# A hybrid encoder block on one Trainium2 core: 128-row attention scores, layer norm statistics ahead of attention, a reordered first norm, and one-hot operations that read their rows from PSUM

## The chip, the cores and the metric

One core of one Trainium2 chip runs the whole kernel as one program. The metric is the device time of one execution in microseconds (us). The engines are TensorE (PE in the profile; PEld is its weight load), VectorE (DVE), ScalarE (ACT), GpSimd (POOL) and SyncE (SP), each with its own instruction queue, worked off in order.

## The reference

For 512 tokens of width 1024, in float32:

```
h = RMSNorm(x);  z = h @ w_in        # columns: GLU 2x1024 | q 16x64 | k 4x64 | v 4x64 | gates 2x1024
A = swish(LayerNorm(conv31(glu)) ) @ w_pw
B = windowed GQA(q, k, v; |t-s| <= 128, ALiBi bias, per-head sink) @ w_o
x = x + (sigmoid(gA) * A + sigmoid(gB) * B) @ w_out
x = x + PEER(RMSNorm(x))             # 8 heads, top 16 of 128 x 128 experts, gelu(u.h) * gate, weighted sum of v rows
out = RMSNorm(x)
```

PEER takes, per token and head, the top 16 of 128 first keys and of 128 second keys, then the top 16 of their sums; each winner is one of 16384 experts.

## The kernel before

**Number format.** Each float32 operand of a projection is split into a high part (ScalarE copy, `split`, L57) and a remainder (L58, on DVE or POOL), and each product is three matmuls (`mm3`, L63 to L65).

**First norm (L140 to L154).** A hand-ordered section: ScalarE, VectorE and SyncE keep program order. Four 128-token tiles of x are loaded; ScalarE takes each sum of squares, VectorE the reciprocal and the scaling; the first weight block is loaded and split; ScalarE loads the sigmoid table; then `spread` transposes on TensorE into `psn` and writes hT as high (ACT L102) and low part (DVE L103).

**Branches (L189 to L331).** `glu(i)` makes two projections into the two PSUM buffers `s` of pool `psa`, which lies where `psn` lay. `conv` is 31 multiply-adds per pair of channel blocks on VectorE. The key tiles `kh`, `kl` hold two key groups each, one in rows 0 to 63 and one in rows 64 to 127. `attend(g, b)` is called 16 times (4 groups, 4 query blocks): per head a score product of 64 contraction rows (L264), maximum and bias (L267), exponentials (ACT L275), division by the denominator (DVE L285 for two heads, ACT L283 for two), transposes (L290), and the product with v (`o`). `fill` puts gate projections between them.

**Layer norm of the convolution (L333 to L355)** follows attention: means by matmul with `ones` (L337), centring (L342), squares (ACT L344), variance by matmul (L345), Sqrt, reciprocal over 512 columns (L348), scaling (DVE L350), Silu (ACT L352), split. Then the projections with w_o, w_pw and w_out (`oraw`).

**PEER.** `u_block(i)` loads 128 experts' u rows, splits them (ACT, POOL `ulo`) and makes 24 matmuls of 384 columns into `hps`; 30 of them (`LEAD`) run ahead of the second half. Meanwhile VectorE does the top-k. `build(t)`, for three of the four token tiles, turns the chosen pairs into a dense gate matrix: indices and gates are transposed into `tp`, written as 2-byte pairs into `tt`, and for each 8 tokens VectorE makes `oij` (2048 columns, compare with an iota, L607) and `ohl` (two multiplies of 1024 columns, L609), from which 16 matmuls make two `gp` tiles (L615, L616), evicted by ScalarE (L618) and written to DRAM. There are 3 x 16 such steps. Afterwards `v_block(i)` combines hidden values and v rows for all 128 expert blocks, with the remaining u blocks and, for token tile 0, 256 row gathers beside it.

**Order.** Outside the hand-ordered sections a planner orders each engine's instructions by dependencies, program order and its own cost estimates; `tc.high_priority()` moves an instruction forward. [...]

Of the kernel before, what the change touches and what calls it, by code (L numbers as in the profile page):

```python
# [44 lines left out]
def encoder_block(ctx, tc, x, g1, w_in, taps, dwb, lng, lnb, w_pw, sink, w_o, w_out, g2, g2row,  # L45
# [71 lines left out]
    with ExitStack() as fc:  # L117
# [15 lines left out]
        with ExitStack() as x0c:  # L133
            x0 = x0c.enter_context(tc.tile_pool(name="x0", bufs=1))
            hT_hi, hT_lo = bigtile(), bigtile()
            psn = x0c.enter_context(tc.tile_pool(name="psn", bufs=6, space=PSUM))
            xt, xs = [], []
            vec = {"g1": const.tile([P, KD], F32, name="g1")}
            ordered = {mybir.EngineType.Activation, mybir.EngineType.DVE, mybir.EngineType.SP}
            with tc.manual_schedule(engines=ordered):  # L140
                ACT.activation(warm, epst, AF.Sqrt)
                for t in range(NT):
                    a = x0.tile([P, D], F32, name="xt", bufs=NT)
                    (SP if t % 2 else ACT).dma_start(a, x[t * P:(t + 1) * P, :])
                    xt.append(a)
                SP.dma_start(vec["g1"], g1)
                for t in range(NT):
                    xn = x0.tile([P, D], F32, name="xn", bufs=NT)
                    rs = rstd_of(xt[t], sm, xn)
                    scale_row(xn, xt[t], rs)  # L150
                    xs.append(xn)
                first = weights(w_in[0])
                ACT.activation(warm, rs, AF.Sigmoid)
                spread(xs, vec["g1"], psn, hT_hi, hT_lo, 0)  # L154
            for name, src in (("dwb", dwb), ("lng", lng), ("lnb", lnb), ("g2", g2)):
                vec[name] = const.tile([P, KD], F32, name=name)
                POOL.dma_start(vec[name], src)
            tapt = const.tile([P, KD, TAPS], F32, name="tapt")
            POOL.dma_start(tapt, taps)
            sinkt = const.tile([P, NH], F32, name="sinkt")  # L160
            POOL.dma_start(sinkt, bcast(sink, NH))
            keyt = const.tile([P, 2, NKEY], F32, name="keyt")
            POOL.dma_start(keyt, keys)
# [12 lines left out]
        with ExitStack() as ac:  # L176
            kvp = ac.enter_context(tc.tile_pool(name="kvp", bufs=1))
            kh = kvp.tile([P, 2, S], F32R, name="kh")
            kl = kvp.tile([P, 2, S], F32R, name="kl")
            vh = kvp.tile([P, NT, 2 * P], F32R, name="vh")  # L180
            vl = kvp.tile([P, NT, 2 * P], F32R, name="vl")
            dist = kvp.tile([P, 3 * P], F32, name="dist")
            aw = ac.enter_context(tc.tile_pool(name="aw", bufs=2))
            psa = ac.enter_context(tc.tile_pool(name="psa", bufs=2, space=PSUM))
# [4 lines left out]
            def glu(i):  # L189
                pa = proj(w_in[i], hT, first if i == 0 else None, ps=psa.tile([P, S], F32, name="s"))  # L190
                pg = proj(w_in[8 + i], hT, ps=psa.tile([P, S], F32, name="s"))
# [23 lines left out]
            for i in range(2):  # L215
                ps = proj(w_in[24 + i], hT)
                with tc.high_priority():
                    split(kh[:, i, :], kl[:, i, :], ps, DVE)
            vps = psa.tile([P, 2, 2, P], F32, name="pt", bufs=2)
            vps2 = psa.tile([P, 2, 2, P], F32, name="pt", bufs=2)  # L220
            vt = []
            for i in range(2):
                ps = proj(w_in[26 + i], hT)
                a = aw.tile([P, 4, 3 * P], F32, name="L", bufs=3).rearrange("p a b -> p (a b)")[:, :S]
                ACT.activation(a, ps, AF.Copy)
# [27 lines left out]
            def attend(g, b):  # L253
# [8 lines left out]
                for i in range(4):  # L262
                    s_ps = psa.tile([P, S], F32, name="s")
                    mm3(s_ps[:, :n], [(qh[rows, gp * 4 + i, cols], ql[rows, gp * 4 + i, cols])],  # L264
                        [(kh[rows, gp, k0 * P:k1 * P], kl[rows, gp, k0 * P:k1 * P])])
                    h = 4 * g + i
# [14 lines left out]
                for i in range(4):  # L281
                    if i % 2:
                        ACT.activation(L[:, i, :n], L[:, i, :n], AF.Copy, scale=rd[:, i:i + 1])  # L283
                    else:
                        DVE.tensor_scalar(L[:, i, :n], L[:, i, :n], rd[:, i:i + 1], None, op0=OP.mult)  # L285
                o_ps = pso.tile([P, 4, P], F32, name="o")
# [12 lines left out]

            dtmp = aw.tile([P, 4, 3 * P], F32, name="L", bufs=3)[:, 0, :]  # L300
            POOL.iota(dist, pattern=[[-1, 3 * P]], base=P, channel_multiplier=1,
# [22 lines left out]
            fill(2)  # L324
            glup.close()
            pso = ac.enter_context(tc.tile_pool(name="pso", bufs=1, space=PSUM))
            for g in range(4):
                make_bias(g)
                for b in range(NT):
                    attend(g, b)  # L330
                    if b == 1 or (g, b) == (0, 3):  # L331
                        fill(1)
            lnp = ac.enter_context(tc.tile_pool(name="lnp", bufs=2))  # L333
            ac_hi, ac_lo = bigtile(), bigtile()
            mu_ps = pso.tile([P, S], F32, name="ln")
# [11 lines left out]
            ACT.activation(rs, var, AF.Sqrt, bias=epst)  # L347
            DVE.reciprocal(rs, rs)  # L348
            for k in range(KD):
                DVE.tensor_tensor(cv[:, k, :], cv[:, k, :], rs, op=OP.mult)  # L350
                act = lnp.tile([P, S], F32, name="act", bufs=2)
                ACT.activation(act, cv[:, k, :], AF.Silu, scale=vec["lng"][:, k:k + 1],  # L352
# [93 lines left out]
    with ExitStack() as rc:  # L446
# [374 lines left out]
```

## Time and profile before

| | us |
|---|---|
| median of 3 runs | 1814.74 (1811.3 to 1815.37) |
| the profiled execution | 1812.98 |
| its span in the trace | 1811.2 |

Busy shares of the span: PE 96%, PEld 82%, DVE 79%, POOL 53%, ACT 43%. A matmul's record is longer than the distance to the next one, since matmuls overlap; a full PE share therefore does not say that PE runs at its peak, and the distance from start to start is what a matmul costs in a dense row. "Idle before" names what ended an engine's wait. PEclk (and the column of that name in the table by stretches) is the granted TensorE clock as a share of full speed.

### The profile page before, as it was taken

What the parts mean: (1) busy time and instruction counts of PE and PEld (TensorE: products, weight loads), DVE (VectorE), ACT (ScalarE), POOL (GpSimd) and SP (SyncE); (2) the same over time, 40 slices, a digit from 0 to 9 for tenths busy, and PEclk for the clock granted to TensorE, in tenths of its full rate; (3) what the DMA queues carried; (4) which work ended last, traced back from release to release, by engine and by line L of the source; (5) the groups of instructions that cost most, each with busy time, mean ns of one, the idle gap of its engine ahead of it and who ended that gap; (6) DMA issues with size and microseconds to landing.
All of it is one profiled execution on the core that took longest, in us unless ns stands there. A gap on an engine that the chain in (4) does not pass through costs nothing.

```text
span 1811.2 us, 25192 instructions
## 1 busy us (share of the span) xinstructions
PE 1734.4 (96%) x8873; PEld 1484.2 (82%) x8873; DVE 1432.8 (79%) x2545; ACT 770.8 (43%) x1374; POOL 961.4 (53%) x741
## 2 busy tenths in 40 slices
PE   6999999989999978888999999999999999999998
PEld 5778877658888877767899999999999999999876
DVE  4999856674536999999989987887787777878874
ACT  4233257883343335555443433333333333333243
POOL 4444421020134445445448888778777778778511
PEclk8999999999999989999999999999999999999999
DMA  4223210024243113777878988888888888898972
GB/s 142 87 92 100 98 59 24 24 82 152 81 148 100 56 59 124 233 214 227 290 257 321 333 309 328 311 318 312 313 317 304 323 317 315 295 332 287 343 259 93
DMA packets 148942, 379.42 MB, mean 209 GB/s; under 512 B 11520, under 2 KB 63760, under 8 KB 148816
## 3 DMA queue, kind: packets, MB, share of 16 engines
q1 hardware_dynamic: 110832, 241.20, 38.1%
q0 software_dynamic: 37120, 134.52, 20.8%
q10 hardware_dynamic: 864, 2.10, 0.3%
q8 instruction: 69, 1.13, 0.2%
q14 instruction: 57, 0.47, 0.1%
HBM read 346.84 MB, written 30.93 MB: 209 GB/s over the span
## 4 chain that ended last, share of the span: by engine, by line
PE 68%; DVE 15%; issue 2%; DMA 2%; ACT 1%; POOL 1%; SPq 0%; POOLq 0%; DVEq 0%; ACTq 0%
PE acc L64 8%; PE acc L63 8%; PE acc L65 8%; PE hps L65 7%; PE hps L64 7%; PE hps L63 7%; PE mm L63 5%; PE mm L65 5%; PE mm L64 4%; DVE ohl L609 4%; DVE oij L607 3%; DMA row<-in_v_dram,eidx 1%; PE s L63 1%; PE pt L290 1%; PE s L64 1%
## 5 line engine op out<-in xcount | busy, mean ns | idle before, releaser
L58 POOL TENSOR_TENSOR ulo<-uraw,uhi 128x512 fp32r<-128x512 f32 x256 | 406.1, 1595 | 290.6 <-ACT uhi L57 271.0
L63 PE MATMUL hps<-big,uhi 128*128 128x384 f32 x1024 | 349.3, 341 | 2.2 <-ACT hb L442 2.1
L65 PE MATMUL hps<-big,ulo 128*128 128x384 f32 x1024 | 349.4, 341 | 0.9 <-POOL ulo L58 0.9
L64 PE MATMUL hps<-big,uhi 128*128 128x384 f32 x1024 | 349.0, 341 | 0.0
L64 PE MATMUL acc<-vlo,ph 128*128 128x512 f32 x768 | 300.7, 392 | 1.6 <-DVE vlo L58 1.6
L65 PE MATMUL acc<-vhi,pl 128*128 128x512 f32 x768 | 299.6, 390 | 0.0
L63 PE MATMUL acc<-vhi,ph 128*128 128x512 f32 x768 | 299.1, 391 | 0.4 <-ACT vhi L57 0.4
L58 POOL TENSOR_TENSOR wlo<-wraw,whi 128x512 fp32r<-128x512 f32 x120 | 157.8, 1318 | 203.5 <-ACT whi L57 202.0
L57 ACT ACTIVATE uhi<-uraw 128x512 fp32r<-128x512 f32 x256 | 160.1, 631 | 233.6 <-PE hps L64 140.9
L643 DVE SCALAR_TENSOR_TENSOR row<-row,h2tok 128x1024 f32<-128x1024 f32 x128 | 189.5, 1487 | 66.4 <-DMA row<-in_u_dram,eidx 66.3
L654 DVE SCALAR_TENSOR_TENSOR yacc<-row,dots,yacc 128x1024 f32<-128x1024 f32 x127 | 177.2, 1396 | 69.7 <-DMA row<-in_v_dram,eidx 69.4
L58 DVE TENSOR_TENSOR vlo<-vraw,vhi 128x1024 fp32r<-128x1024 f32 x128 | 188.6, 1474 | 18.9 <-ACT vhi L57 18.9
L636 POOL DMA_INDIRECT row<-in_u_dram,eidx x128 | 183.8, 1436 | 33.2 <-issue 21.1
L63 PEld LDWEIGHTS hps<-big,uhi 128*128 128x128 f32 x1024 | 194.3, 190 | 6.6 <-ACT hb L442 2.5
L64 PEld LDWEIGHTS hps<-big,uhi 128*128 128x128 f32 x1024 | 194.6, 190 | 4.2
L57 ACT ACTIVATE whi<-wraw 128x512 fp32r<-128x512 f32 x152 | 95.3, 631 | 239.2 <-PE mm L64 125.5
L65 PEld LDWEIGHTS hps<-big,ulo 128*128 128x128 f32 x1024 | 194.2, 190 | 2.0 <-POOL ulo L58 1.9
L636 POOL DMA_INDIRECT row<-in_v_dram,eidx x128 | 165.1, 1290 | 48.7 <-DVE yacc L654 21.5
L57 ACT ACTIVATE ph<-hb 128x384 fp32r<-128x384 f32 x128 | 66.8, 523 | 287.4 <-PE acc L64 274.6
L65 PEld LDWEIGHTS acc<-vhi,pl 128*128 128x128 f32 x768 | 144.2, 188 | 30.9 <-DVE pl L58 0.3
L64 PEld LDWEIGHTS acc<-vlo,ph 128*128 128x128 f32 x768 | 144.2, 188 | 30.0 <-DVE vlo L58 3.7
L63 PEld LDWEIGHTS acc<-vhi,ph 128*128 128x128 f32 x768 | 144.1, 188 | 28.4 <-ACT vhi L57 1.0
(221 smaller groups left out, 3211.7 us busy)
## 6 DMA issues: line engine op xcount, KB each, us to landing
uraw<-in_ut_dram SPq DMA_DIRECT2D x128, 512.0 KB
vraw<-in_v_dram SPq DMA_DIRECT2D x128, 512.0 KB
gates_dram<-st SPq DMA_DIRECT2D x12, 2048.0 KB
gt<-gates_dram SPq DMA_DIRECT2D x32, 768.0 KB
wraw<-in_w_in_dram SPq DMA_DIRECT2D x44, 512.0 KB
wraw<-in_w_query_dram SPq DMA_DIRECT2D x16, 512.0 KB
wraw<-in_w_o_dram SPq DMA_DIRECT2D x8, 512.0 KB
oraw<-in_w_out_dram SPq DMA_DIRECT2D x16, 256.0 KB
```

The lines of the kernel that those rows point to most:

```text
L57: ACT.activation(hi, src, AF.Copy)
L58: lo_engine.tensor_tensor(lo, src, f(hi), op=OP.subtract)
L63: PE.matmul(ps, wh, mh, start=first and i == 0, stop=False)
L64: PE.matmul(ps, wh, ml, start=False, stop=False)
L65: PE.matmul(ps, wl, mh, start=False, stop=last and i == n - 1)
L290: PE.transpose(pt[:, i, :], L[:, i, j * P:(j + 1) * P], ident)
L607: DVE.tensor_tensor(prs(oij), iota8, rows(0), op=OP.is_equal)
L609: DVE.tensor_tensor(prs(ohl)[:, s * TB8:(s + 1) * TB8], prs(oij)[:, TB8:], rows(2)[:, s * TB8:(s + 1) * TB8], op=OP.mult)
L636: POOL.indirect_dma_start(out=row, out_offset=None, in_=table, in_offset=bass.IndirectOffsetOnAxis(ap=eidx[:, c:c + 1], axis=0))
L643: DVE.scalar_tensor_tensor(row, row, 1.0, h2tok, op0=OP.mult, op1=OP.mult, accum_out=dots[:, c:c + 1])
L654: DVE.scalar_tensor_tensor(yacc, row, dots[:, c:c + 1], yacc, op0=OP.mult, op1=OP.add)
```

## The change

- First norm: the fourth tile's sum of squares goes to VectorE; the three others, all roots, the reciprocals and the scalings are written in another order; the split of the first weight block is put into the transpose loop after steps 1 and 4 and the sigmoid table load after it; the first projection goes to the pool `psm`.
- Keys: `kh`, `kl` get one slot of 128 rows for each of the four groups, the other group's 64 rows are zeroed by POOL, and the score products contract over 128 rows. The key split becomes two of 64 rows each.
- Two of four divisions per `attend` go from ACT to POOL. The pool `aw` (score and bias tiles) is opened after the convolution.
- The layer norm's statistics go ahead of attention; its scaling (8 tiles) goes to POOL, between the calls of `attend` for g = 1 and 2. Silu writes in place.
- `build`: ScalarE copies `tt` bit by bit into a PSUM tile `tq`; `oij` and `ohl` read their rows there; `ohl` is one operation of 2048 columns. [...]

```diff
@@ first norm
-                for t in range(NT):
-                    xn = x0.tile([P, D], F32, name="xn", bufs=NT)
-                    rs = rstd_of(xt[t], sm, xn)
-                    scale_row(xn, xt[t], rs)
-                    xs.append(xn)
-                first = weights(w_in[0])
-                ACT.activation(warm, rs, AF.Sigmoid)
-                spread(xs, vec["g1"], psn, hT_hi, hT_lo, 0)
...
+                DVE.scalar_tensor_tensor(xs[3], xt[3], 1.0, xt[3], op0=OP.mult, op1=OP.mult, accum_out=sss[3])
+                raw0 = wst.tile([P, KD, P], F32, name="wraw", bufs=3)
+                SP.dma_start(raw0.rearrange("p k c -> p (k c)"), w_in[0])
+                for t in (0, 1, 2, 3):
+                    if t < 3:
+                        ACT.activation(xs[t], xt[t], AF.Square, accum_out=sss[t])
+                    ACT.activation(sss[t], sss[t], AF.Sqrt, scale=1.0 / D, bias=epst)
...
+                for k in range(KD):
+                    tp = psn.tile([P, S], F32, name="mm")
...
+                    if k in (1, 4):
...
+                        split(hi, lo, raw0[:, q * n:(q + 1) * n, :], POOL)
...
+                ACT.activation(warm, epst, AF.Sigmoid)
@@ keys and scores
-            kh = kvp.tile([P, 2, S], F32R, name="kh")
-            kl = kvp.tile([P, 2, S], F32R, name="kl")
+            kh = kvp.tile([P, 4, S], F32R, name="kh")
+            kl = kvp.tile([P, 4, S], F32R, name="kl")
+            for a in (kh, kl):
+                POOL.memset(f(a[64:, 0::2, :]), 0.0)
+                POOL.memset(f(a[:64, 1::2, :]), 0.0)
...
-                pa = proj(w_in[i], hT, first if i == 0 else None, ps=psa.tile([P, S], F32, name="s"))
+                pa = (proj(w_in[0], hT, first) if i == 0 else
+                      proj(w_in[i], hT, ps=psa.tile([P, S], F32, name="s")))
...
-                    split(kh[:, i, :], kl[:, i, :], ps, DVE)
+                    for r in range(2):
+                        rr = slice(64 * r, 64 * r + 64)
+                        split(kh[rr, 2 * i + r, :], kl[rr, 2 * i + r, :], ps[rr], DVE)
...
-                    mm3(s_ps[:, :n], [(qh[rows, gp * 4 + i, cols], ql[rows, gp * 4 + i, cols])],
-                        [(kh[rows, gp, k0 * P:k1 * P], kl[rows, gp, k0 * P:k1 * P])])
+                    mm3(s_ps[:, :n], [(qh[:, gp * 4 + i, cols], ql[:, gp * 4 + i, cols])],
+                        [(kh[:, g, k0 * P:k1 * P], kl[:, g, k0 * P:k1 * P])])
...
-                    if i % 2:
-                        ACT.activation(L[:, i, :n], L[:, i, :n], AF.Copy, scale=rd[:, i:i + 1])
-                    else:
-                        DVE.tensor_scalar(L[:, i, :n], L[:, i, :n], rd[:, i:i + 1], None, op0=OP.mult)
+                    (POOL if i % 2 else DVE).tensor_scalar(L[:, i, :n], L[:, i, :n], rd[:, i:i + 1], None,
+                                                           op0=OP.mult)
@@ layer norm: L335 to L348 now stand ahead of this loop
+            def ln_scale(k):
+                POOL.tensor_tensor(cv[:, k, :], cv[:, k, :], rs, op=OP.mult)
...
+                    attend(g, b)
+                    if g in (1, 2):
+                        ln_scale(4 * (g - 1) + b)
...
-                DVE.tensor_tensor(cv[:, k, :], cv[:, k, :], rs, op=OP.mult)
@@ build
-            tp = psg.tile([P, 3, P], F32, name="tp", bufs=1)
+            tp = psg.tile([P, 4, P], F32, name="gp", bufs=4)
...
+            tq = psg.tile([P, 512], F32, name="tq", bufs=2)
+            ACT.activation(tq, tt.rearrange("p g s t b -> p (g s t b)").bitcast(F32), AF.Copy)
+            tqv = tq.bitcast(F16).rearrange("p (g s t b) -> p g s t b", s=4, t=TB8, b=2)
...
-                        a = tt[:, n // TB8, s:s + 2].rearrange("p s t b -> p (s t) b")
+                        a = tqv[:, n // TB8, s:s + 2].rearrange("p s t b -> p (s t) b")
...
-                    for s in range(2):
-                        DVE.tensor_tensor(prs(ohl)[:, s * TB8:(s + 1) * TB8], prs(oij)[:, TB8:],
-                                          rows(2)[:, s * TB8:(s + 1) * TB8], op=OP.mult)
+                    jj = oij[:, 1].rearrange("p t (a b) -> p t a b", b=2)
+                    DVE.tensor_tensor(ohl.rearrange("p s t (a b) -> p s t a b", b=2),
+                                      jj[:, None].to_broadcast([P, 2, TB8, NKEY // 2, 2]),
+                                      rows(2).rearrange("p (s t) a b -> p s t a b", s=2), op=OP.mult)
...
-                        gp = psg.tile([P, 4, NKEY], F32, name="gp", bufs=5)
+                        gp = psg.tile([P, 4, NKEY], F32, name="gp", bufs=4)
```

## Rows read from the trace of the kernel before

**Rows 1.** The page, busy time by engine, and its costliest POOL group of the weight splits.

```profile
PE 1734.4 (96%) x8873; PEld 1484.2 (82%) x8873; DVE 1432.8 (79%) x2545; ACT 770.8 (43%) x1374; POOL 961.4 (53%) x741
...
L58 POOL TENSOR_TENSOR wlo<-wraw,whi 128x512 fp32r<-128x512 f32 x120 | 157.8, 1318 | 203.5 <-ACT whi L57 202.0
```

**Rows 2.** Busy time by stretch: start:end, length, each engine's busy time (count), clock, DMA.

```profile
243.00:367.40 124.40, 124.36 (x579) 87.18 (x578) 80.99 (x265) 98.43 (x238) 9.05 (x7) 1.00 0.08 26
367.40:406.80 39.40, 33.35 (x126) 21.32 (x124) 29.92 (x48) 34.19 (x67) 10.51 (x8) 0.96 0.31 94
...
685.00:855.00 170.00, 140.30 (x1233) 118.18 (x1232) 169.88 (x261) 86.97 (x166) 79.25 (x47) 0.98 0.65 199
855.00:875.00 20.00, 19.59 (x112) 18.95 (x110) 19.30 (x76) 11.13 (x19) 10.92 (x11) 1.00 1.04 348
1000.00:1200.00 200.00, 200.00 (x1014) 182.33 (x1013) 172.61 (x201) 75.57 (x120) 165.91 (x113) 1.00 0.87 320
```

**Rows 3.** Timeline of the start, ScalarE: start, length, line, operation, count.

```profile
14.79 4.71 ACT L102 ACTIVATE big<-mm,g 128x512 fp32r<-128x512 f32 x8
```

**Rows 4.** Timeline of the start, TensorE: the first projection's first matmul.

```profile
20.91 0.79 PE L63 MATMUL s<-big,whi 128*128 128x512 f32 x1 [2.64 <-DVE big L103]
```

**Rows 5.** Timeline of TensorE in attention: the first and the last run of 64-row scores.

```profile
243.46 0.38 PE L63 MATMUL s<-kh,qh 64*128 64x256 f32 x1
...
363.20 0.40 PE L64 MATMUL mm<-ql,whi 128*128 128x512 f32 x1
363.44 0.43 PE L63 MATMUL o<-ph,vh 128*128 128x512 f32 x1
363.80 0.38 PE L63 MATMUL s<-kh,qh 64*128 64x256 f32 x1
364.02 0.28 PE L64 MATMUL s<-kl,qh 64*128 64x256 f32 x1
...
364.49 0.27 PE L65 MATMUL s<-kh,ql 64*128 64x256 f32 x1
364.69 0.50 PE L65 MATMUL mm<-qh,wlo 128*128 128x512 f32 x1
365.04 0.40 PE L64 MATMUL o<-pl,vh 128*128 128x512 f32 x1
```

**Rows 6.** Timeline of VectorE after attention: the layer norm's reciprocal.

```profile
392.37 3.35 DVE L348 RECIPROCAL rs<-rs 128x512 f32<-128x512 f32 x1 [5.62 <-ACT rs L347]
```

**Rows 7.** Groups by line from 685 to 855 us, VectorE (busy us, mean ns | idle before).

```profile
L609 DVE TENSOR_TENSOR ohl<-oij,tt 128x1024 f16<-128x1024 f16 x96 | 83.6, 912 | 0.0
L607 DVE TENSOR_TENSOR oij<-iotar,tt 128x2048 f16<-128x2048 f16 x48 | 69.7, 1457 | 0.0
```

**Rows 8.** Groups by line from 685 to 855 us, TensorE.

```profile
L615 PE MATMUL gp<-oij,ohl 128*128 128x128 f16 x384 | 54.3, 223 | 24.6 <-DVE ohl L609 24.5
```

**Rows 9.** Timeline of TensorE in a build: two `gp` matmuls, the first and twelfth of a row.

```profile
780.33 0.22 PE L615 MATMUL gp<-oij,ohl 128*128 128x128 f16 x1
...
780.94 0.22 PE L615 MATMUL gp<-oij,ohl 128*128 128x128 f16 x1
```

**Rows 10.** Timeline of VectorE in a build.

```profile
770.66 1.21 DVE L607 TENSOR_TENSOR oij<-iotar,tt 128x2048 f16<-128x2048 f16 x1
...
773.29 3.44 DVE L607 TENSOR_TENSOR oij<-iotar,tt 128x2048 f16<-128x2048 f16 x2
```

**Rows 11.** Timeline of GpSimd in the same stretch.

```profile
773.55 2.10 POOL L58 TENSOR_TENSOR ulo<-uraw,uhi 128x512 fp32r<-128x512 f32 x1 [0.74 <-ACT uhi L57]
```

**Rows 12.** Groups by line and shape over the span, VectorE.

```profile
L209 DVE SCALAR_TENSOR_TENSOR ca<-ub,tapt,ca 128x512 f32<-128x512 f32 x232 | 159.3, 752 | 1.5
...
L508 DVE TENSOR_REDUCE ij<-oh 128x128 f32<-128x2048 f16 x8 | 18.1, 2268 | 0.0
...
L404 DVE TENSOR_TENSOR sg<-mm,sg 128x512 f32<-128x512 f32 x8 | 5.5, 692 | 14.1 <-PE mm L65 14.1
...
L405 DVE TENSOR_TENSOR sg<-sg,sg 128x512 f32<-128x512 f32 x8 | 5.5, 689 | 0.1
```

More of the change, by code (lines that the diff above doesn't have):

```diff
@@ L136, in encoder_block @@
             psn = x0c.enter_context(tc.tile_pool(name="psn", bufs=6, space=PSUM))
-            xt, xs = [], []
+            xt = []
             vec = {"g1": const.tile([P, KD], F32, name="g1")}
@@ L146, in encoder_block @@
                 SP.dma_start(vec["g1"], g1)
-                for t in range(NT):
-                    xn = x0.tile([P, D], F32, name="xn", bufs=NT)
-                    rs = rstd_of(xt[t], sm, xn)
-                    scale_row(xn, xt[t], rs)
-                    xs.append(xn)
-                first = weights(w_in[0])
-                ACT.activation(warm, rs, AF.Sigmoid)
-                spread(xs, vec["g1"], psn, hT_hi, hT_lo, 0)
+                xs = [x0.tile([P, D], F32, name="xn", bufs=NT) for _ in range(NT)]
+                sss = [sm.tile([P, 1], F32, name="ss") for _ in range(NT)]
+                DVE.scalar_tensor_tensor(xs[3], xt[3], 1.0, xt[3], op0=OP.mult, op1=OP.mult, accum_out=sss[3])
[5 more added lines that the diff above has]
+                    ACT.activation(sss[t], sss[t], AF.Sqrt, scale=1.0 / D, bias=epst)
+                for t in range(NT):
+                    rs = sm.tile([P, 1], F32, name="rs")
+                    DVE.reciprocal(rs, sss[t])
+                    scale_row(xs[t], xt[t], rs)
+                first = []
+                for k in range(KD):
+                    tp = psn.tile([P, S], F32, name="mm")
+                    for i, xn in enumerate(xs):
+                        PE.transpose(tp[:, i * P:(i + 1) * P], xn[:, k * P:(k + 1) * P], ident)
+                    ACT.activation(hT_hi[:, k, :], tp, AF.Copy, scale=vec["g1"][:, k:k + 1])
+                    DVE.scalar_tensor_tensor(hT_lo[:, k, :], tp, vec["g1"][:, k:k + 1], f(hT_hi[:, k, :]),
+                                             op0=OP.mult, op1=OP.subtract)
+                    if k in (1, 4):
+                        n = KD // 2
+                        q = k // 4
+                        hi = wst.tile([P, n, P], F32R, name="whi", bufs=4)
+                        lo = wst.tile([P, n, P], F32R, name="wlo", bufs=4)
+                        split(hi, lo, raw0[:, q * n:(q + 1) * n, :], POOL)
+                        first += [(hi[:, m, :], lo[:, m, :]) for m in range(n)]
+                ACT.activation(warm, epst, AF.Sigmoid)
             for name, src in (("dwb", dwb), ("lng", lng), ("lnb", lnb), ("g2", g2)):
@@ L182, in encoder_block @@
             dist = kvp.tile([P, 3 * P], F32, name="dist")
-            aw = ac.enter_context(tc.tile_pool(name="aw", bufs=2))
             psa = ac.enter_context(tc.tile_pool(name="psa", bufs=2, space=PSUM))
@@ L223, in encoder_block @@
                 ps = proj(w_in[26 + i], hT)
-                a = aw.tile([P, 4, 3 * P], F32, name="L", bufs=3).rearrange("p a b -> p (a b)")[:, :S]
+                a = gl.tile([P, S], F32, name="sgm")
                 ACT.activation(a, ps, AF.Copy)
@@ L298, in attend @@
                 split(qh[rows, gp * 4:gp * 4 + 4, cols], ql[rows, gp * 4:gp * 4 + 4, cols], o_ps[rows], DVE)
-            dtmp = aw.tile([P, 4, 3 * P], F32, name="L", bufs=3)[:, 0, :]
+            dtmp = gl.tile([P, S], F32, name="sgm")[:, :3 * P]
             POOL.iota(dist, pattern=[[-1, 3 * P]], base=P, channel_multiplier=1,
@@ L325, in encoder_block @@
             glup.close()
+            aw = ac.enter_context(tc.tile_pool(name="aw", bufs=2))
             pso = ac.enter_context(tc.tile_pool(name="pso", bufs=1, space=PSUM))
[L327 to L332, printed above, removed]
             lnp = ac.enter_context(tc.tile_pool(name="lnp", bufs=2))
-            ac_hi, ac_lo = bigtile(), bigtile()
             mu_ps = pso.tile([P, S], F32, name="ln")
@@ L348, in encoder_block @@
             DVE.reciprocal(rs, rs)
+            def ln_scale(k):
+                POOL.tensor_tensor(cv[:, k, :], cv[:, k, :], rs, op=OP.mult)
+            for g in range(4):
+                make_bias(g)
+                for b in range(NT):
+                    attend(g, b)
+                    if g in (1, 2):
+                        ln_scale(4 * (g - 1) + b)
+                    if b == 1 or (g, b) == (0, 3):
+                        fill(1)
+            ac_hi, ac_lo = bigtile(), bigtile()
             for k in range(KD):
-                DVE.tensor_tensor(cv[:, k, :], cv[:, k, :], rs, op=OP.mult)
-                act = lnp.tile([P, S], F32, name="act", bufs=2)
+                act = cv[:, k, :]
                 ACT.activation(act, cv[:, k, :], AF.Silu, scale=vec["lng"][:, k:k + 1],
```

## The prediction

> **What bounds the kernel now.** I read the page first: TensorE is busy for 1734 of 1811 us [rows 1], so only work taken from TensorE, or waits of TensorE, can move the end. Then the table of busy time by stretch, to see where that share hides slack. From 875 us on TensorE is full with 1014 matmuls in 200 us [rows 2]; the change touches nothing there, so that phase should only start earlier and pass every gain on. Slack lies in three places. At the start TensorE's first projection begins at 20.91 us [rows 4]. Around the end of attention it is idle for 39.40 - 33.35 = 6.05 us, with the clock at 0.96 [rows 2]. And from 685 to 855 us VectorE is busy for 169.88 of 170.00 us while TensorE's records cover 140.30 [rows 2], with 24.5 us of waiting for `ohl` [rows 8]: VectorE sets the pace of the builds. A fourth place is hidden in full records: in attention TensorE is busy for 124.36 of 124.40 us [rows 2], but the timeline shows irregular distances between starts [rows 5].
>
> **The change, part by part.** The sum is made against the profiled execution, 1812.98 us (span 1811.2 and 1.78 around it); the median of the runs shown is 1814.74, 1.76 more.
>
> *Start.* ScalarE's first eviction of hT is at 14.79 us and eight take 4.71, 0.59 each [rows 3]. Ahead of it in the queue now stand one square, two weight copies of that size and a table load; the square goes to VectorE, the others behind the first evictions, so evictions start some 2 us earlier, and with the two copies among them end about 1 us earlier. The first projection waits 2.64 us more for VectorE's last hT subtraction [rows 4], because its PSUM buffer lies where the transposes' buffers lay. In `psm` it needs only block k = 0 and can follow the transposes at once. 1.3 + 2.64 = 4 us gained. VectorE's new sum of squares stands ahead of its reciprocals but runs beside ScalarE's first squares; were it late, everything behind it on VectorE would be, about 1 us. SyncE's order of loads stays (x, g1, first weights). Bounds: 0 to 5 gained.
>
> *128-row scores.* Within a run of 64-row scores over 256 columns, starts are 0.12 apart (four steps from 364.02 to 364.49), between 128-row matmuls of 512 columns 0.24 (363.20 to 363.44) [rows 5]. Going in, `o` to `s` takes 0.36 and the first score 0.22; going out, the last score takes 0.20 (364.49 to 364.69) and the next 128-row matmul 0.35 [rows 5]. The excess is 0.12 + 0.10 + 0.08 + 0.11 = 0.41 for this run, 0.40 for the middle one of all. There are 49 such runs from 243.46 to 363.80, the first and the last shown [rows 5]: 49 x 0.40 = 19.6 us. Changes of weights, of PSUM tile or of operand between 128-row matmuls show no such excess, only changes of the row count do. A 128-row score streams the same columns, so I price it at the 64-row distance and take the full 19.6; bounds 0 (the gap has another cause) to 21. It counts only while TensorE remains the bound: ScalarE is busy for 98.43 of 124.40 there [rows 2]. The 32 divisions that leave it cost up to an eviction's 0.59 each [rows 3], so it falls to about 80.
>
> *Divisions and scalings on POOL.* No row shows a tensor_scalar on POOL. The nearest is the two-input split of 512 columns at 1318 ns [rows 1], 2.6 ns per column, so at most 0.99 us for 384 columns and 0.66 for 256: 32 divisions take at most 26 us, 8 layer norm scalings 10.5. POOL is busy for 9.05 of 124.40 us there [rows 2], so 46 us fit. A division waits for VectorE's `rd`; behind it on POOL stand the splits of the next gate weights, for which TensorE's fill projections wait. Three score tiles rotate, so one block's division runs beside the next block's scores: taken as 0; without that cover 16 x 1.6 = 26 us lost.
>
> *Keys.* Two more copies and two more subtractions of up to 0.69 (L405) [rows 12] run beside 232 multiply-adds of 0.752 [rows 12], a per cent of VectorE's work there, and four POOL memsets run before the keys exist. Taken as 0, bounds 0 to 2.8 lost.
>
> *Layer norm.* The same matmuls, squares and centring move ahead of attention; nothing is saved on TensorE. At the end of attention the reciprocal of 3.35 us [rows 6] and the scalings behind it no longer delay VectorE's w_o splits and Silu: of the 6.05 idle us I take 5 back. Late next is the last block's softmax chain, which has less work to hide it since the statistics' matmuls are gone. At the head the reciprocal stands in VectorE's queue ahead of the maxima of the first scores, of which only two PSUM tiles exist: 3 us lost. Net 2 gained; bounds 6 gained to 4 lost.
>
> *Builds.* From 685 to 855 us the one-hot operations take 69.7 + 83.6 = 153.3 us of VectorE's time for 48 steps, 3.19 each [rows 7]. An undisturbed `oij` takes 1.21 us; two that coincide with a POOL split take 3.44 [rows 10], and that split 2.10 [rows 11]: the two engines hold each other up. The convolution's multiply-adds, which read one operand in SBUF and the accumulator in PSUM, average 752 ns for 512 columns beside POOL's splits [rows 12], with no such stretching. So with rows in PSUM I expect no holding up. What a PSUM operand of 2 bytes costs no row shows. [...] I take 1.21: at equal pace the operand's place is worth nothing (L404 with a PSUM input 692 ns, L405 without 689 [rows 12]).
>
> [...]
>
> Two operations a step are then 96 x 1.21 = 116 us, 37 less. VectorE's stretch would be 170 - 37 = 133. But TensorE is next: of its 1233 matmuls 768 are `gp` and 6 transposes, so 459 are of the u blocks. Those cost 19.59 / 112 = 0.175 in the dense stretch that follows [rows 2], the `gp` 0.61 / 11 = 0.055 [rows 9]: 80.3 + 42.2 + 1 and the 19.6 from 855 to 875 are 143 us of the present 190. The gain is thus at most 47, by TensorE. I add 15 us of waits: of the 24.5 that it spends today on `ohl` [rows 8] some remain at the head of each build, where three bit copies of about 0.6 are new on ScalarE (behind each stand u splits and evictions), the `gp` tiles are four instead of five, and the next build's transposes wait for one. 190 - 158.5 = 31.5 us gained; bounds 47 gained to 96 x 2.27 - 153.3 = 65 lost. The gate writes use the DMA engines at 0.65 [rows 2], 0.75 after, not yet the limit.
>
> *Sum.* 4 + 19.6 + 2 + 31.5 = 57.1: 1812.98 - 57.1 = 1755.9, against the median 1757.6. I predict 1758.
>
> **Rivals.**
> [...] Chance 0.13.
>
> *TensorE's order or the DMA takes the builds' gain.* u loads stand in SyncE's queue with the 2 MB gate writes, and from 855 to 875 the DMA share is 1.04 [rows 2]; if only half is realized, 16 of 31.5, the time is 1773. Against it: 0.65 on average before. Chance 0.12.
>
> *Attention becomes ScalarE's or latency-bound, or the excess isn't the rows'.* Only 8 of 19.6 us are realized: 1769; with nothing 1777, the change then not doing what it says. For it: ScalarE's 98 of 124 us, and POOL's longer divisions. Against it: the excess appears at 49 of 49 changes of row count. Chance 0.13.
>
> *Forecast.* Chance 0.62, by itself 1743 to 1772.
>
> **How the numbers follow.** The forecast and the two partial rivals lie in 1738 to 1792 with most of their 0.87; what is left out is mainly the slow-pace rival at 1854 and the corners. About 0.2%, 3.6 us, is what a measurement of this kernel can tell from no change. Faster: 0.62 + 0.12 + 0.13 = 0.87, less 0.01 for a sum of half gains that meets a mid price near 1.86 us: 0.86. Same 0.02, slower 0.12.
>
> **What would show it.** Right: the first projection before 18 us; no distances above 0.30 around scores, and 128-row scores at 0.12 and 0.175; no reciprocal between attention and the w_o products; `oij` and `ohl` at about 1.2 us each, 48 of both, whatever POOL does; TensorE dense from the builds on, the steady phase beginning near 820 us. Wrong: one-hot operations of 2.2 us; gaps around scores as before; TensorE waiting for divisions on POOL; the u blocks' loads late in the builds.

## The result, and the profile after

The changed kernel takes 1794.59 us (median of 4 runs, 1792.38 to 1797.08) against 1813.28 for the kernel before (4 runs, 1811.3 to 1815.37): ratio 0.9894, 95% interval 0.9879 to 0.9908. It is faster by 18.7 us, a third of the 57 us forecast. The profiled execution has a span of 1790.6 us.

The page's line of busy time of the changed kernel, which answers to [rows 1]:

```profile
PE 1715.0 (96%) x8873; PEld 1491.1 (83%) x8873; DVE 1397.3 (78%) x2493; ACT 767.0 (43%) x1351; POOL 985.5 (55%) x785
```

And its table by stretch, as [rows 2] (start:end, length, busy time of each engine with its count, granted clock, DMA share, GB/s):

```profile
243.70:376.40 132.70, 115.08 (x566) 87.05 (x564) 95.91 (x271) 107.54 (x238) 49.61 (x42) 0.97 0.04 13
376.40:440.00 63.60, 57.89 (x241) 45.03 (x241) 32.21 (x54) 27.95 (x55) 16.41 (x12) 0.95 0.46 157
692.00:837.00 145.00, 141.07 (x1301) 133.10 (x1300) 144.09 (x263) 94.99 (x179) 60.70 (x57) 0.99 0.79 244
837.00:860.00 23.00, 10.69 (x65) 10.38 (x62) 21.50 (x82) 8.29 (x15) 9.93 (x11) 0.84 0.96 331
985.00:1185.00 200.00, 200.00 (x1015) 182.47 (x1014) 167.15 (x199) 75.78 (x121) 167.34 (x111) 1.00 0.86 315
```

Three things are to be seen. In the score stretch TensorE, full before (124.36 of 124.40), now sits idle for 132.70 - 115.08 = 17.6 us. In the builds it is nearly full (141.07 of 145.00, where it was 140.30 of 170.00). Behind the builds, from 837 to 860 us, 12.3 of 23 us are idle. From 985 us on TensorE is full, as it was before.

Places in the trace, by the start of the named matmul, of the two kernels and of the runs below (`acc` is the sum that the matmuls of the v blocks build up, so its first matmul begins the last phase):

| us | first projection | first score | last projection | first `acc` | last `acc` |
|---|---|---|---|---|---|
| before | 20.91 | 243.46 | 640.08 | 875.20 | 1803.07 |
| changed | 17.10 | 243.66 | 645.25 | 859.98 | 1782.48 |
| e1 | 17.28 | 243.71 | 640.92 | 855.85 | 1777.89 |
| e2 | 17.05 | 237.13 | 636.76 | 851.04 | 1772.30 |
| e3 | 16.91 | 236.99 | 622.49 | 836.89 | 1759.67 |
| e4 | 17.01 | 236.92 | 637.24 | 852.23 | 1774.49 |
| e5 | 17.17 | 237.31 | 624.31 | 859.35 | 1785.40 |
| e9 | 20.89 | 243.09 | 629.41 | 844.41 | 1768.30 |

The start gained 3.8 us at the first projection, but attention, where 21.6 were to be gained, lost: the last projection comes 5.2 us later than before. Only the builds and what follows brought the time down.

What was forecast for the scores and the one-hot operations, taken singly, held. The scores on 128 rows stand among other matmuls at their own distance (timeline of TensorE, changed kernel, 384 columns; against [rows 5], of 256 columns, 0.36 in, 0.35 out and 0.22 for the first):

```profile
303.59 0.34 PE L63 MATMUL s<-kh,qh 128*128 128x384 f32 x1
303.77 0.34 PE L64 MATMUL s<-kl,qh 128*128 128x384 f32 x1
303.94 0.40 PE L63 MATMUL o<-ph,vh 128*128 128x512 f32 x1
304.18 0.34 PE L65 MATMUL s<-kh,ql 128*128 128x384 f32 x1
```

0.18 and 0.17 for a score, 0.24 for the `o` between. The one-hot operations, with their rows in PSUM, run at 1.21 and 1.20 us on average, the time of an undisturbed `oij` before [rows 10], and GpSimd's splits beside them aren't stretched (1.29 us on average, against 2.10; groups by line from 692 to 837 us, of VectorE and then of GpSimd; against [rows 7, 11]):

```profile
L639 DVE TENSOR_TENSOR oij<-iotar,tq 128x2048 f16<-128x2048 f16 x48 | 58.2, 1213 | 0.2 <-PE gp L649 0.2
L641 DVE TENSOR_TENSOR ohl<-oij,tq 128x2048 f16<-128x2048 f16 x48 | 57.7, 1202 | 0.0
```

```profile
L58 POOL TENSOR_TENSOR ulo<-uraw,uhi 128x512 fp32r<-128x512 f32 x46 | 59.0, 1287 | 80.4 <-ACT uhi L57 76.7 <-ACT st L651 3.4 <-DMA uraw<-in_ut_dram 0.3
```

What went wrong stands in TensorE's waits from 236 to 440 us (who waited <- for whom: total, times, longest), in its timeline and in that of GpSimd:

```profile
PE pt L314 <- POOL L L308: 12.5, 19, 1.6
PE pt L314 <- DVE L L308: 3.2, 4, 1.3
```

```profile
350.87 0.71 PE L314 MATMUL pt<-ident,L 128*128 128x128 f32 x5
352.04 0.44 PE L314 MATMUL pt<-ident,L 128*128 128x128 f32 x2 [0.46 <-POOL L L308]
353.41 0.33 PE L314 MATMUL pt<-ident,L 128*128 128x128 f32 x1 [0.93 <-POOL L L308]
```

```profile
263.51 1.31 POOL L368 TENSOR_TENSOR cv<-cv,rs 128x512 f32<-128x512 f32 x1
264.81 1.87 POOL L308 TENSOR_SCALAR L<-L,rd 128x256 f32<-128x256 f32 x2
266.65 6.25 POOL L368 TENSOR_TENSOR cv<-cv,rs 128x512 f32<-128x512 f32 x5
```

The transposes of heads 1 and 3 wait for GpSimd's divisions (in the kernel before no transpose waits for a division), one after the other, in block after block; and the layer norm's scalings stand in the same queue. On ScalarE (timeline, changed kernel) two table loads and a square root stand ahead of the first exponential, which comes 12.5 us after the first score (in run e3 below, 3.1 after it):

```profile
252.91 1.28 ACT L365 ACT_TABLE_LOAD   x1
254.20 0.69 ACT L365 ACTIVATE rs<-ln,epst 128x512 f32<-128x512 f32 x1
254.91 1.28 ACT L301 ACT_TABLE_LOAD   x1
256.20 0.51 ACT L301 ACTIVATE L<-L,nm 128x256 f32<-128x256 f32 x1
```

Three theories followed: A, the divisions on GpSimd; B, the layer norm's place; C, that the 128-row scores gain nothing.

### The profile page after: what moved, and what is told of

It is laid out like the page before. It is cut to its first block, busy times and chain, and to the rows that moved or that the text cites. A ratio compares the mean times of both kernels' runs of the same rounds, so it can differ in the third digit from the quotient of the medians.

```text
span 1790.6 us, 25210 instructions
## 1 busy us (share of the span) xinstructions
PE 1715.0 (96%) x8873; PEld 1491.1 (83%) x8873; DVE 1397.3 (78%) x2493; ACT 767.0 (43%) x1351; POOL 985.5 (55%) x785
## 4 chain that ended last, share of the span: by engine, by line
PE 72%; DVE 8%; DMA 3%; ACT 3%; issue 2%; POOL 2%; SPq 0%; POOLq 0%; DVEq 0%; ACTq 0%
PE hps L64 9%; PE hps L65 9%; PE hps L63 9%; PE acc L64 8%; PE acc L63 8%; PE acc L65 8%; PE mm L63 4%; PE mm L64 4%; PE mm L65 4%; DMA vraw<-in_v_dram 1%; PE gp L648 1%; PE gp L649 1%; POOL L L308 1%; DMA row<-in_v_dram,eidx 1%; PE pt L314 1%
## 5 line engine op out<-in xcount | busy, mean ns | idle before, releaser
L58 POOL TENSOR_TENSOR ulo<-uraw,uhi 128x512 fp32r<-128x512 f32 x256 | 380.9, 1496 | 293.6 <-ACT uhi L57 284.6
L63 PE MATMUL acc<-vhi,ph 128*128 128x512 f32 x768 | 300.2, 391 | 12.3 <-ACT vhi L57 12.3
L676 DVE SCALAR_TENSOR_TENSOR row<-row,h2tok 128x1024 f32<-128x1024 f32 x128 | 177.5, 1392 | 77.3 <-DMA row<-in_u_dram,eidx 76.8
L687 DVE SCALAR_TENSOR_TENSOR yacc<-row,dots,yacc 128x1024 f32<-128x1024 f32 x127 | 183.9, 1448 | 61.0 <-DMA row<-in_v_dram,eidx 60.8
L669 POOL DMA_INDIRECT row<-in_v_dram,eidx x128 | 170.8, 1335 | 49.4 <-DVE yacc L687 19.7
```

What stands on the lines that cost most here:

```text
L58: lo_engine.tensor_tensor(lo, src, f(hi), op=OP.subtract)
L63: PE.matmul(ps, wh, mh, start=first and i == 0, stop=False)
L669: POOL.indirect_dma_start(out=row, out_offset=None, in_=table, in_offset=bass.IndirectOffsetOnAxis(ap=eidx[:, c:c + 1], axis=0))
L676: DVE.scalar_tensor_tensor(row, row, 1.0, h2tok, op0=OP.mult, op1=OP.mult, accum_out=dots[:, c:c + 1])
L687: DVE.scalar_tensor_tensor(yacc, row, dots[:, c:c + 1], yacc, op0=OP.mult, op1=OP.add)
```

## Experiments

Each run was timed in five rounds beside the kernel before, in four groups whose medians for that kernel are 1814.6 us (e1 to e4), 1811.4 (e5 to e8), 1813.9 (e9 to e11) and 1815.1 (e12). Between groups the ratios therefore compare better than the medians. Half-widths of the ratios' intervals are 0.0014 to 0.0019, some 3 us; for a difference of two runs that makes some 4 us.

**e1: divisions back on ScalarE.**

```diff
-                    (POOL if i % 2 else DVE).tensor_scalar(L[:, i, :n], ...)
+                    if i % 2:
+                        ACT.activation(L[:, i, :n], L[:, i, :n], AF.Copy, scale=rd[:, i:i + 1])
+                    else:
+                        DVE.tensor_scalar(L[:, i, :n], ...)
```

> The changed kernel with one edit: the divisions of heads 1 and 3 of each attend go from GpSimd back to ScalarE. Theory A (the GpSimd divisions, 1.34 us for 384 columns, lengthen the chain of each attend; TensorE waited 12.5 us for them in 19 waits): about 12 us less than the changed kernel, 1782 us, and no transpose of attention waits for GpSimd. Theory B (the layer norm's place ahead of attention is what cost: late first exponential, table swaps, nothing to fill the end): the waits move to VectorE or ScalarE and the time stays within 3 us of 1794.6. Theory C (128-row scores give nothing) says nothing on this run.

Measured 1786.25 us, ratio 0.9841 [0.9826, 0.9855]: 8.3 less than the changed kernel. No transpose waits for GpSimd, as A said; but part of the waiting moved. At the end of attention (timeline of e1, TensorE and then ScalarE):

```profile
379.95 0.63 PE L65 MATMUL o<-ph,vl 128*128 128x512 f32 x1
387.88 0.79 PE L63 MATMUL mm<-qh,whi 128*128 128x512 f32 x1 [7.30 <-ACT whi L57]
```

```profile
382.40 1.28 ACT L391 ACT_TABLE_LOAD   x1
383.69 3.62 ACT L391 ACTIVATE sg<-sg 128x4096 f32<-128x4096 f32 x1
387.21 2.17 ACT L57 ACTIVATE whi<-wraw 128x512 fp32r<-128x512 f32 x4
```

ScalarE reaches the w_o weights behind a sigmoid of 3.62 us, and no layer norm matmul is left to cover it. A is right with two thirds of its size; waits for ScalarE, as B said, are there too, so B is not refuted.

**e2: layer norm late, divisions on GpSimd.** The statistics, reciprocal and scalings (on VectorE) return behind the last attend, where Silu then stands too.

```diff
             for g in range(4):
                 ...
-                    if g in (1, 2):
-                        ln_scale(4 * (g - 1) + b)
+            mu_ps = pso.tile([P, S], F32, name="ln")      # statistics as above, now here
+            ...
             for k in range(KD):
+                DVE.tensor_tensor(cv[:, k, :], cv[:, k, :], rs, op=OP.mult)
```

> The changed kernel with the layer norm where it was before (means, squares, reciprocal, scalings on VectorE and Silu after the last attend), divisions left on GpSimd. Theory A (GpSimd divisions): the layer norm gains or costs little, 1791 to 1797 us. Theory B (the layer norm's place): the first exponential comes 12 us earlier after the first score, the table loads of the stretch fall from 13 to about 7, and the time falls to about 1782 us.

Measured 1782.49 us, 0.9829 [0.9811, 0.9846]: 12.1 less. B holds as well, and GpSimd's wait stays (waits of e2, 236 to 440 us; and its GpSimd timeline, one attend):

```profile
PE pt L314 <- POOL L L308: 13.1, 22, 1.0
```

```profile
298.71 2.59 POOL L308 TENSOR_SCALAR L<-L,rd 128x384 f32<-128x384 f32 x2 [8.74 <-DVE rd L306]
```

**e3: both edits; e4: both, and 64-row scores.** e4 has kh and kl as [P, 2, S] with one split each, and

```diff
-                    mm3(s_ps[:, :n], [(qh[:, gp * 4 + i, cols], ql[:, gp * 4 + i, cols])],
-                        [(kh[:, g, k0 * P:k1 * P], kl[:, g, k0 * P:k1 * P])])
+                    mm3(s_ps[:, :n], [(qh[rows, gp * 4 + i, cols], ql[rows, gp * 4 + i, cols])],
+                        [(kh[rows, gp, k0 * P:k1 * P], kl[rows, gp, k0 * P:k1 * P])])
```

> The changed kernel with both edits: divisions on ScalarE and the layer norm after attention; 128-row scores stay. Theories A and B, each with its own share, and the 128-row scores worth what was forecast (19.6 us): the last projection at about 616 us and 1766 us in all. Theory C (the 128-row scores give nothing, the switches' time comes back as waits): attention as long as before the change, last projection at about 636 us, 1786 us in all.

> The kernel of the run with both edits, with the scores back on 64 rows as well, so that attention is that of the kernel before and only the start and the one-hot builds are new. If the 128-row scores are worth 19.6 us, this run is that much longer than the one with both edits: 1786 against 1766 us. If they are worth nothing (theory C), the two are equal within 2 us. In either case this run measures the start and the builds alone: 1813.3 - 3.8 - 26 = about 1783.5 us by the milestones of the two traces, 1778 us by the forecast terms (4 and 31.5).

Measured: e3 1768.69 us, 0.9744 [0.973, 0.9758]; e4 1782.82, 0.9828 [0.9813, 0.9842]. The two edits together take back 25.9 us; the 128-row scores are worth 14.1, so C falls, but not 19.6. In e3 all waits of TensorE for divisions are gone but 0.9 us (waits of e3, the lines that name them):

```profile
PE mm L63 <- DVE sg L392: 4.4, 2, 3.5
...
PE pt L316 <- ACT L L309: 0.7, 1, 0.7
...
PE pt L316 <- DVE L L311: 0.2, 1, 0.2
```

In e4 the 49 unbroken runs of score matmuls have mean distances of 0.314 (in), 0.260 (first), 0.243 (last) and 0.341 us (out); the 53 runs of e3 have 0.189, 0.200, 0.175 and 0.249. That is 0.345 less a run, 16.9 us over 49. From the first score to the last projection e3 is 14.8 us shorter; 0.6 us more of idle time stands against it, and the rest of the difference isn't accounted for. The keys' term, taken as 0, held: the first score is at 236.92 us in e4, with the old keys, and at 236.99 in e3.

**e5: the old builds in e3; e6: only the rows back in SBUF.** e5 has the function `build` of the kernel before. e6 keeps two operations a step:

```diff
-            tq = psg.tile([P, 512], F32, name="tq", bufs=2)
-            ACT.activation(tq, tt.rearrange("p g s t b -> p (g s t b)").bitcast(F32), AF.Copy)
-                        a = tqv[:, n // TB8, s:s + 2].rearrange("p s t b -> p (s t) b")
+                        a = tt[:, n // TB8, s:s + 2].rearrange("p s t b -> p (s t) b")
```

> The kernel of the run with both edits (1768.7 us), with the one-hot builds of the kernel before: rows read from SBUF, three one-hot operations a step, five gate tiles. The difference is what the builds' change alone is worth. Forecast term: 31.5 us, so 1800 us. By the milestones of the traces (20.1 us from the last projection to the first accumulation, 5.6 after it): 1794.5 us. If a part of the change in the builds' time came from the front instead, less than 20 us and under 1789.

> The kernel of the run with both edits (1768.7 us), whose one-hot operations read their rows from SBUF again, still two operations a step and four gate tiles. Theory H (VectorE and GpSimd hold each other up where all operands lie in SBUF): the comparison averages about 1.45 us instead of 1.21 and the product about 1.7, VectorE again needs some 150 us for them, GpSimd's splits average well above 1.4 us, and the time is 1788 to 1795 us. Theory O (one operation less a step is what gained, the place of the rows is indifferent): both at about 1.2 us and the time within 3 us of 1768.7.

Measured: e5 1795.32 us, 0.9907 [0.9889, 0.9924]; e6 1798.07, 0.9924 [0.9907, 0.9941]. The builds' change is worth 26.6 us by the medians, 29.6 by the ratios, and one operation less a step gives none of it by itself: with the rows in SBUF the kernel is no faster than with the old builds. Rows in PSUM with the old three operations were not run. Theory H holds (groups of e6: VectorE's from 640 to 865 us, GpSimd's from 685 to 855):

```profile
L636 DVE TENSOR_TENSOR ohl<-oij,tt 128x2048 f16<-128x2048 f16 x48 | 75.5, 1591 | 0.0
L634 DVE TENSOR_TENSOR oij<-iotar,tt 128x2048 f16<-128x2048 f16 x48 | 69.4, 1453 | 1.0 <-PE gp L644 1.0
```

```profile
L58 POOL TENSOR_TENSOR ulo<-uraw,uhi 128x512 fp32r<-128x512 f32 x39 | 78.1, 2009 | 72.6 <-ACT uhi L57 69.4 <-PE hps L65 3.2
```

The same operations take 1.21 and 1.20 us in e3, and GpSimd's split 1.29 instead of 2.01.

**e7: 32 u blocks ahead.**

```diff
-LEAD = 30
+LEAD = 32
-    hring = ctx.enter_context(tc.tile_pool(name="hring", bufs=LEAD + 2))
+    hring = ctx.enter_context(tc.tile_pool(name="hring", bufs=LEAD + 1))
```

> The kernel of the run with both edits (1768.7 us), with 32 u blocks ahead of the accumulation instead of 30 (the ring of their results has one spare tile instead of two). Theory G (TensorE runs out of u blocks while the last gates go to memory and back: 12 us idle between the last u block and the first accumulation): two blocks of 24 matmuls at 0.175 us fill 8.4 us of it, 1760.3 us. Rival (the transfers set the stretch: two more loads push the gates' write and read by as much): 1766 to 1770 us, and the idle stretch stays.

Measured 1767.43 us, 0.9747 [0.973, 0.9765]: no gain. By stretch, e3 and then e7:

```profile
825.00:830.00 5.00, 0.00 (x0) 0.00 (x0) 4.90 (x13) 1.31 (x3) 2.72 (x2) 0.69 0.92 290
830.00:835.00 5.00, 0.00 (x0) 0.00 (x0) 5.00 (x9) 0.57 (x2) 0.00 (x0) 0.50 1.01 406
835.00:840.00 5.00, 3.11 (x7) 2.15 (x8) 4.20 (x8) 4.97 (x8) 0.00 (x0) 0.50 0.64 236
```

```profile
825.00:830.00 5.00, 4.37 (x26) 4.05 (x24) 4.90 (x13) 2.67 (x5) 3.56 (x3) 1.00 0.95 299
830.00:835.00 5.00, 0.00 (x0) 0.00 (x0) 5.00 (x7) 0.00 (x0) 3.56 (x2) 0.92 1.02 412
835.00:840.00 5.00, 1.74 (x4) 1.07 (x5) 5.00 (x11) 4.17 (x7) 0.00 (x0) 0.50 0.57 234
```

The two blocks do run in the gap, but the first `acc` moves from 836.89 to 838.26 us and the last from 1759.67 to 1757.54 only: the time lies in the rival's range. Where the rest of the 8.4 us went is not settled.

**e8: e1 with Silu tied to the last softmax; e12: e8 with the statistics in the middle.** In e8 Silu's scale is a copy of lng to which zero times the last block's `rd` is added, so that the planner can't pull it forward. e12 runs the statistics ahead of the third head group, and the scalings in the third and fourth.

```diff
+            z = lnp.tile([P, 1], F32, name="z", bufs=1)
+            DVE.tensor_scalar(z, last_rd[0][:, 0:1], 0.0, None, op0=OP.mult)
+            lng2 = lnp.tile([P, KD], F32, name="lng2", bufs=1)
+            DVE.tensor_scalar(lng2, vec["lng"], z, None, op0=OP.add)
```

> The changed kernel with the divisions on ScalarE (1786.25 us), the layer norm's statistics and scalings still ahead of and within attention, but the Silu operations made to wait for the last block's softmax (their scale takes part in a product with zero of its reciprocal). Theory S (Silu between the exponentials costs, by table loads of 1.28 us on ScalarE): table loads in the stretch fall from 12 to about 8 and the time to about 1780 us. Theory F (what costs is the head, where the first exponential waits for the statistics, and the end, where no statistics' matmuls are left to run beside the last softmax chains): 1786 to 1791 us, since eight Silu and copies now stand behind attention.

> The run with the tied Silu and divisions on ScalarE (1779.3 us, 0.9818 of the kernel before), with the layer norm's statistics after the second of four head groups instead of ahead of the first, its scalings in the last two groups. What is left of the early layer norm's cost there is 11 to 13 us against the run with the norm late (1768.7 us, 0.9744). Theory Head (the late first exponential and the waits for the first blocks, 6 us by that run's trace, are the greater part): the first exponential comes 4 us after the first score again, 1772 to 1774 us (0.976 to 0.978). Theory End (the 32 statistics' matmuls, 14 us at 0.43, are missing beside the last softmax chains): no more than 2 us gained, 1777 to 1780 us (0.981).

Measured: e8 1779.31 us, 0.9818 [0.98, 0.9837]; e12 1775.05, 0.9785 [0.977, 0.9801]. Theory S has e8's number: 7.0 us less than e1 by the medians, 4.2 by the ratios, and the table loads from 236 to 440 us fell from 12 to 7, the number that e3 has. But its reason isn't shown. TensorE's waits from 236 to 380 us, where Silu stood between the exponentials, hardly change: 12.2 us in e1, 11.6 in e8. What is gone is e1's one wait of 7.30 us for the w_o weights: with the tie the long sigmoid, which stood ahead of them, comes some 28 us earlier, inside attention, with a table load of its own, and TensorE waits 0.97 us at the first w_o product (timeline of e8, ScalarE and then TensorE):

```profile
353.95 1.28 ACT L398 ACT_TABLE_LOAD   x1
355.25 3.63 ACT L398 ACTIVATE sg<-sg 128x4096 f32<-128x4096 f32 x1
```

```profile
384.27 0.74 PE L63 MATMUL mm<-qh,whi 128*128 128x512 f32 x2 [0.97 <-ACT qh L57]
```

The granted clock follows: from 380 to 440 us it is 0.90 in e1 and 1.00 in e8. e12 gained 4.3 us more (6.0 by the ratios), between its two theories and at the edge of what the intervals can tell. The stretches of e8 and then e12:

```profile
243.30:300.00 56.70, 52.13 (x255) 38.46 (x254) 44.08 (x110) 43.30 (x107) 16.54 (x13) 1.00 0.06 19
300.00:383.00 83.00, 74.76 (x381) 57.27 (x379) 60.53 (x187) 75.74 (x174) 1.30 (x1) 0.98 0.08 26
```

```profile
237.00:300.00 63.00, 62.58 (x322) 48.24 (x321) 43.98 (x138) 50.92 (x135) 9.10 (x7) 1.00 0.10 34
300.00:384.00 84.00, 72.22 (x336) 52.54 (x335) 60.79 (x161) 73.03 (x153) 10.97 (x8) 0.96 0.08 26
```

TensorE's 4.6 us of idle time at the head are gone but for 0.4; at the end the idle time is 11.8 us instead of 8.2. There TensorE waits for the last softmax chains (waits of e12, 236 to 440 us, the two greatest):

```profile
PE o L64 <- DVE pl L58: 3.5, 4, 2.6
PE pt L319 <- DVE L L314: 3.2, 3, 2.4
```

What separates e12 from e3, 6.4 us, lies behind 300 us: the first score is at 237.2 us in e12 and 237.0 in e3. Idle time accounts for 3.1 us of it (11.8 from 300 to 384 us in e12, 8.7 from 300 to 440 in e3); the rest isn't settled.

**e9: the old start in e3.** The first norm and the first projection's tile as before (the first two parts of the diff undone).

> The kernel of the run with both edits (1768.7 us, 0.9744 of the kernel before), with the first norm and the first projection's PSUM tile as in the kernel before. The difference is the start's worth alone. Forecast term: 4 us, so 1772.7 us (0.9766). By the milestones (3.9 us earlier at the first projection, 2.8 left at the last projection): 1771.5 us (0.9759). If the head start is lost before attention (VectorE's convolution sets the first stretch): within 1 us of 1768.7.

Measured 1776.81 us, 0.9795 [0.9781, 0.981]: the start is worth 8.1 us by the medians, 9.3 by the ratios, twice what any theory said. The first 20 us of e9 and then of e3:

```profile
10.00:30.00 20.00, 15.09 (x59) 12.01 (x58) 7.28 (x13) 11.47 (x22) 10.45 (x18) 0.83 0.33 124
```

```profile
10.00:30.00 20.00, 17.53 (x83) 14.58 (x84) 9.12 (x18) 11.60 (x23) 8.96 (x8) 1.00 0.38 139
```

The first projection comes 4.0 us earlier and runs at once at a granted clock of 1.00, where e9 has 0.50 in a part of this stretch (from 18.8 to 25.6 us, around waits of 1.6 and 3.3 us; mean 0.83); at the first score the lead is 6.1 us, and at the last projection 6.9.

**e10: all divisions on VectorE; e11: one division on GpSimd.** Both with the layer norm late; in e11 head 1 is divided on ScalarE and head 3 on GpSimd.

```diff
-                    (POOL if i % 2 else DVE).tensor_scalar(L[:, i, :n], ...)
+                    DVE.tensor_scalar(L[:, i, :n], ...)
```

> The kernel of the run with both edits (1768.7 us, 0.9744), with all four divisions of an attend on VectorE (0.34 to 0.38 us each by its trace; ScalarE's took 0.49 to 0.62). Theory P (taking the divisions from ScalarE is worth nothing and costs only by their length on GpSimd): 0.973 to 0.975, within 2 us of 1768.7, and TensorE waits for no division. Theory Q (ScalarE's queue did hold TensorE in the rest of the waits, so that its relief gains where the divisions stay short): 1763 to 1766 us. Theory V (VectorE's maxima wait behind the divisions, and with them the score tiles): 1772 us or more, with waits of scores for VectorE.

> The run with the layer norm late (1782.5 us, 0.9829), with one division of an attend on GpSimd (head 3) instead of two; head 1 goes to ScalarE. Theory L (what costs is the length of GpSimd's chain, two divisions one behind the other, 2.59 us for 384 columns): the chain halves to 1.30 us, of which some 0.5 was ScalarE's anyway, and most of the 13.8 us goes: 1770 to 1773 us (0.976 to 0.977). Theory H (any hand-over to GpSimd costs, or it disturbs VectorE by sharing memory, whatever its length): half of it stays, 1775 to 1777 us (0.979).

Measured: e10 1768.43 us, 0.9749 [0.9733, 0.9765]; e11 1767.71, 0.9744 [0.973, 0.9759]. Theory P holds for the time: taking divisions from ScalarE gains nothing (of its second half, no wait for a division, two waits of 2.2 us in all remain in e10). Theory L, and more than it said: a single division on GpSimd, 1.38 us for 384 columns, costs nothing measurable; only the second one behind it reaches TensorE.

e3, e7, e10 and e11 all beat both kernels by about the same: 1767.4 to 1768.7 us, 26 less than the changed kernel.

## Why the prediction was wrong

| term, us gained | forecast | by the medians | by the ratios | from |
|---|---|---|---|---|
| start | 4 | 8.1 | 9.3 | e9 - e3 |
| 128-row scores | 19.6 | 14.1 | 15.2 | e4 - e3 |
| divisions on GpSimd | 0 | -8.3 to -13.8 | -9.6 to -15.4 | e1 - changed, e3 - e2 |
| layer norm early | 2 | -12.1 to -17.6 | -11.8 to -17.6 | e2 - changed, e3 - e1 |
| both of these | 2 | -25.9 | -27.2 | e3 - changed |
| builds | 31.5 | 26.6 | 29.6 | e5 - e3 |
| sum | 57.1 | 22.9 | 26.9 | 18.7 and 19.2 measured |

The smaller size of each pair is with the other edit still in. A ratio is taken times 1814 us. The sums are 4 and 8 us above the measured ones, within the intervals of four differences. Two slips in the prediction's own sums are small: 143 + 15 is 158, not 158.5, and the start's 1.3 stands where the text ahead of it has about 1.

*Layer norm, the step that failed most.* I counted what leaves the end (the reciprocal of 3.35 us, the scalings: 5 us) and one reciprocal at the head (3 us), and bounded the loss at 4. Three things were not in that count.

- At the head also the squares, a square root and two table loads precede the first exponential (256.20 us). TensorE is idle for 4.6 us there in e8 and for 0.4 in e3.
- At the end the forecast gain did come: e3's waits of 5.5 us around the w_o products (for VectorE's `sg` and `wlo`) are not in e8. But the 32 statistics' matmuls, 0.43 us each, had been TensorE's work beside the last softmax chains (they run from 335 to 389 us in the kernel before). I named these chains as late next and gave them no price: from 300 us on TensorE waits 2.9 us for attention's own operations in e3, 8.9 in e8 and 11.4 in e12.
- ScalarE's order changed. Silu, ready early, stood between the exponentials with table loads of 1.28 us both ways, and the w_o weights stood behind the sigmoid: the 7.30 us of e1.

These don't make up the whole loss. Of the 10.6 us that e8 still takes more than e3, TensorE's waits from 236 to 440 us show 4.8 (13.4 against 8.6); the rest stays open.

*Divisions.* The bound on their length was none: 0.99 us for 384 columns from the nearest row, 1.34 measured. And I took "one block's division runs beside the next block's scores" for cover. Two in a row on GpSimd made 2.59 us (e2); e2's 13.1 us of waits, and none in e11 with one division of 1.4, say that the cover ends somewhere between. The 26 us that I named as the price without cover held the loss, but as a corner; the rival on attention names GpSimd's longer divisions and prices no loss. The relief of ScalarE was worth nothing (e10).

*128-row scores.* The cause was right: in e4 and e3, alike but for the row count of the scores and for the keys, the distances add up to 1.158 and 0.813 us a run. The size was 0.40 for each excursion, against 0.345 as the mean over all; and 14.1 of the 16.9 us that this makes reached the end.

*Start.* Priced to the first projection (4 us; 3.8 to 4.0 found), not to the end. The lower clock of e9 there accounts, by my estimate, for some 2 us more: most of the 11 matmuls from 20.89 us on, at 0.50, start 0.43 us apart, those from 25.70 us on, at 1.00, 0.23; and the lead grows from 4.0 to 6.1 us up to the first score; the other 2 are not accounted for and lie within the intervals.

*Builds.* The pace that I chose, 1.21 us from PSUM, is what ran (1.20 to 1.21 us on average for 2048 columns), so the slow-pace rival, 1854 us, fell. No run shows the 2.27 us of the loss bound for a one-hot operation with its rows in PSUM: it is the time of L508's reduction [rows 12], and the longest one-hot operation of e3 took 1.22 us. TensorE's idle time is 3.9 us in the builds and 12.3 behind them, near the 15 taken, but for another reason than I gave, so that term came out by luck: after the last `gp` the gates go to memory and back, and the u blocks run out before they return. From the last `gp` to the first `acc` it takes 22.2 us in the kernel before, where u blocks fill it, and 23.0 in the changed one, where they end after 10.4. At the end of that gap (855 to 860 us) the clock is at 0.50, which was not in my sum either.

The rival on attention (latency-bound, 1769 or 1777) pointed at the right place, but stopped at no gain, where the stretch from the first to the last projection lost 9 us (table above).

## What to carry to other kernels

An operation moved off the path takes its cover role with it: before moving work, list what else was waiting beside it, and price the place where it arrives by the first result needed there, table loads included. Two short operations in a row on one engine are one long latency, here 2.59 us for two divisions on GpSimd; look at what one of them costs before both are moved. Bundled edits can hide each other's loss: here 26 of 49 us gained were given away by two of the parts, and undoing them one at a time showed it. And a run whose time fits a theory has not shown its reason: e8 has theory S's time, but the wait that vanished is another.

## Not expected of the hardware

A comparison or product of 2-byte values by VectorE beside GpSimd's splits averages 1.45 to 1.59 us with all inputs in SBUF (e6) and 1.20 to 1.21 with one of the two in PSUM (e3); GpSimd's split falls from 2.01 to 1.29. Both engines' operations are longer together (of VectorE's in e6 the median is 1.21 us and the longest takes 2.31), and neither is once one of VectorE's inputs has left SBUF (longest 1.22 in e3); by what means one holds up the other is not shown. In attention too VectorE's division of 384 columns, which has one tensor as input, averages 612 ns beside GpSimd's (e2) and 480 ns without (e3, where one of 16 took 1448); that this has the same cause is not shown.

TensorE's granted clock falls within some of its pauses: 0.69 and then 0.50 in the two 5-us stretches after e3's last u block, and 0.50 from 380 to 388 us in e1, around the 7.3-us wait. In e9 matmuls of 512 columns start 0.43 us apart where it is 0.50 (up to 25.33 us) and 0.23 where it is 1.00 (from 25.70 us on).
